# Strassen's form for the first MLP product of layer 0, in a kernel of a two-layer diffusion trunk

## The chip, the cores and the metric

The kernel runs on one core of one Trainium2 chip. The metric is the device time of one execution in microseconds, as the median of the runs. Five engines work side by side, each through its own list of instructions in order: TensorE (PE: matmuls, with its weight loads as PEld), VectorE (DVE), ScalarE (ACT), GpSimd (POOL) and SyncE (SP), which here only issues DMAs. They wait for each other by semaphores.

## The reference

Two layers work on 512 noised tokens and 256 context tokens of 1024 features, all in float32. Each layer has a modulated norm, a combined input projection, a gated mixer and attention, an output projection with a gated residual, and then the MLP:

```python
def sqrelu_mlp(h, w1, w2):
    return jnp.square(jax.nn.relu(h @ w1)) @ w2
...
        x_lat = x_lat + ga2 * sqrelu_mlp(modulate(rmsnorm(x_lat, norm2_g[l]), sh2, sc2),
                                         w_ff1[l], w_ff2[l])
```

`w1` is 1024 x 4096 and `w2` 4096 x 1024. Layer 0 does the same for the context tokens. Layer 1, the last one, needs of the context only its keys and values, so of the context's six modulation vectors it uses only the first two (`csh1`, `csc1`). The output is the noised stream.

## The kernel before

**Number format.** Every float32 operand of a matmul is split into a high part (rounded by an ACT cast) and a low part (the rest, a subtraction). A product is three passes: high x high, high x low, low x high. `split` (lines 206 to 208) does this for a source: `act.copy` on line 207, the subtraction on DVE, or where it is named on POOL, on line 208. Nearly all matmuls go through the helper `mm`, whose matmul is on line 203.

**Layout.** Features lie on the 128 partitions and tokens on the free axis: `X` is the residual stream, `h2[k]` (k = 0 to 7) the normed tokens of a layer's MLP as [128, high/low, 768]. A hidden tile `H[m]` (m = 0 to 31) has the same shape. The tile framework gives each tile a buffer of its tag's pool: units `A0` to `A7`, `B0` to `B6`, `C0`, `C1` and `X0` to `X3` with one buffer each, small temporaries `w` and `s` with three each, and in PSUM `pa` (two banks wide), `pb` and `pt` (one bank), two buffers each. A tile waits for the last reader of the buffer that it takes over.

**Weights.** `pump` (line 224) loads blocks of [128, 1024] through SP (line 242) into two `raw` buffers, in the order that `block_order` (line 120) lists, and splits them into a ring of four pairs of buffers `hi` and `lo`. `take` hands out the next block; `release` lets the ring go on some time later.

**The MLP.** `ff1_first` (line 963) makes hidden tiles 0 to 3, the context's tokens ahead of the noised ones. `ff1(m)` (line 986) makes one hidden tile: two token parts of 384 columns, each 8 feature blocks x 3 passes, 48 matmuls in all. `relu2` (line 951) then takes ReLU and square on ACT (lines 954 and 959) and square and low half on DVE (lines 960 and 961). The second product, `proj4` (line 786), adds four hidden tiles to all 8 output tiles in a chunk: 8 x 2 parts x 12 matmuls. DVE adds each result, times a gate, to `X` (line 784). `steady` (line 1012) runs eight chunks: for `ch` below 7 first `ff1(ch*4+4)`, then the second product of chunk `ch`, then the other three tiles of the next chunk. So a hidden tile of the next chunk stands on PE between the last tile of a chunk and the chunk's second product.

**Beside it**, in layer 0's MLP, `mod_wide` (line 347) computes layer 1's modulation without PE: 12 chunks of 512 columns, each 8 feature blocks for two conditions. ACT scales a block (lines 365 and 368), POOL adds it up (line 369), DVE transposes and reduces (lines 380 and 381), and four small matmuls (line 386) end the sum. `more()` advances it in small steps between the pieces of the MLP. `consts(l)` (line 550) loads a layer's constants and makes the rotary tables times the gains (`G`, lines 563 and 564); for layer 1 it is called right after layer 0's `ff1_first`.

**Order.** The program is written along an emission clock (`Flow`), which counts PE's time and emits delayed work when due. What each engine then runs in which order is chosen by the framework's scheduler from its own cost model, except where a manual region keeps the written order. In layer 0's MLP, chunks 0 to 6 are in such a region for DVE and ACT (`PAR["FM0"] = 'DA'`); layer 1's MLP is in the scheduler's order throughout.

```python
        if eng:
            with tc.manual_schedule(engines=eng):
                steady(range(PAR["FC"]))
            with region('ffz%d' % l):
                steady(range(PAR["FC"], 8))
        else:
            steady(range(8))
```

## Time and profile before

| what | value |
|---|---|
| median of 3 runs | 1532.02 us (1531.33 to 1533.99) |
| profiled execution, its own time: the span from its first to its last instruction | 1530.9 us |
| PE busy | 1484.1 us (97%), 8804 matmuls |
| DVE, ACT, POOL busy | 957.4 (63%), 682.6 (45%), 402.0 (26%) us |
| mean granted PE clock | 0.993 |
| moved by DMA | 148.83 MB, mean 97 GB/s |

The profile gives one execution, and no time for it but its span; what lies around the span is seen only by comparing it with the runs. Instructions are grouped by the line that issues them, the engine, the operation and the names of the tiles that they write and read (`lo<-raw,hi`). A group shows its count, its busy time in us, the mean of one in ns, and after the last bar how long the engine was idle before them and whom it waited for. The chain that ended last is followed back from the last instruction, at each step to what released it. A busy PE need not be PE at its peak, since matmuls are pipelined: the distance between the starts of matmuls tells more than their listed length.

### The profile page before, as it was taken

What the parts mean: (1) busy time and instruction counts of PE and PEld (TensorE: products, weight loads), DVE (VectorE), ACT (ScalarE), POOL (GpSimd) and SP (SyncE); (2) the same over time, 40 slices, a digit from 0 to 9 for tenths busy, and PEclk for the clock granted to TensorE, in tenths of its full rate; (3) what the DMA queues carried; (4) which work ended last, traced back from release to release, by engine and by line L of the source; (5) the groups of instructions that cost most, each with busy time, mean ns of one, the idle gap of its engine ahead of it and who ended that gap; (6) DMA issues with size and microseconds to landing.
All of it is one profiled execution on the core that took longest, in us unless ns stands there. A gap on an engine that the chain in (4) does not pass through costs nothing.

```text
span 1530.9 us, 22786 instructions
## 1 busy us (share of the span) xinstructions
PE 1484.1 (97%) x8804; PEld 1321.5 (86%) x8804; DVE 957.4 (63%) x1874; ACT 682.6 (45%) x1142; POOL 402.0 (26%) x362
## 2 busy tenths in 40 slices
PE   6999899999999999999999999998999999999998
PEld 2899686779899999999999998996889888888887
DVE  5868966776855555555555547988796644444443
ACT  3542355564545453545444424535784433322221
POOL 0112320023244545545454603035213000000000
PEclk9999999999999999999999999999999999999999
DMA  9221324321134333333333321221101333332332
GB/s 359 67 74 48 119 91 152 110 83 56 62 108 122 113 123 126 111 118 106 124 109 124 98 68 56 86 80 44 41 1 56 97 96 97 98 97 97 96 98 79
DMA packets 49948, 148.83 MB, mean 97 GB/s; under 512 B 5424, under 2 KB 6832, under 8 KB 49840
## 3 DMA queue, kind: packets, MB, share of 16 engines
q1 hardware_dynamic: 49264, 146.46, 29.9%
q8 instruction: 69, 1.13, 0.3%
q10 hardware_dynamic: 576, 0.92, 0.2%
q14 instruction: 39, 0.32, 0.1%
HBM read 145.26 MB, written 2.10 MB: 96 GB/s over the span
## 4 chain that ended last, share of the span: by engine, by line
PE 82%; DVE 12%; DMA 2%; ACT 2%; issue 1%; POOL 0%; SPq 0%; ACTq 0%; POOLq 0%; DVEq 0%
PE pa L203 51%; PE pb L203 21%; PE pt L844 3%; PE pt L203 3%; PE pb L326 2%; DVE lo L208 1%; DMA X<-in_xT 1%; DMA C<-in_w_mod 1%; DVE X L784 1%; DMA A<-in_w_mod 1%; DVE m L277 1%; PE pt L626 1%; DVE B L961 1%; ACT hi L207 1%; PE pb L865 0%
## 5 line engine op out<-in xcount | busy, mean ns | idle before, releaser
L203 PE MATMUL pa<-A,hi 128*128 128x384 f32 (+2 forms) x1696 | 449.2, 347 | 1.7 <-ACT w L954 0.6
L207 ACT CAST hi<-raw 128x1024 fp32r<-128x1024 f32 x171 | 179.5, 1050 | 409.9 <-PE pa L203 326.3
L208 DVE TENSOR_TENSOR lo<-raw,hi 128x1024 fp32r<-128x1024 f32 x155 | 202.7, 1308 | 215.8 <-ACT hi L207 212.4
L203 PEld LDWEIGHTS pa<-A,hi 128*128 128x128 f32 x1696 | 304.7, 188 | 25.9 <-ACT w L954 1.8
L369 POOL TENSOR_TENSOR C<-C,s 128x512 f32<-128x512 f32 x168 | 240.5, 1463 | 245.0 <-ACT s L368 244.8
L203 PE MATMUL pa<-A,lo 128*128 128x384 f32 (+2 forms) x848 | 293.4, 347 | 1.1 <-DVE lo L208 1.1
L203 PE MATMUL pa<-B,hi 128*128 128x384 f32 (+1 forms) x900 | 246.4, 356 | 4.4 <-DVE X L784 4.4
L203 PEld LDWEIGHTS pa<-B,hi 128*128 128x128 f32 x900 | 162.9, 188 | 21.5 <-DVE X L784 9.2
L784 DVE SCALAR_TENSOR_TENSOR X<-pa,modT,X 128x384 f32<-128x384 f32 (+1 forms) x168 | 88.0, 547 | 143.0 <-PE pa L203 143.0
L203 PEld LDWEIGHTS pa<-A,lo 128*128 128x128 f32 x848 | 159.3, 188 | 12.0 <-DVE lo L208 1.3
L203 PE MATMUL pa<-B,lo 128*128 128x384 f32 (+1 forms) x450 | 158.1, 353 | 0.0
L203 PE MATMUL pb<-B,hi 128*128 128x256 f32 (+2 forms) x600 | 152.3, 340 | 0.4 <-DVE X L784 0.4
L368 ACT ACTIVATE s<-k,silu 128x512 f32<-128x512 f32 x168 | 114.3, 716 | 49.4 <-DMA k<-in_w_mod 27.3
L203 PE MATMUL pb<-hi,A 128*128 128x256 f32 x672 | 126.1, 285 | 0.0
L784 DVE SCALAR_TENSOR_TENSOR X<-pb,modT,X 128x512 f32<-128x512 f32 (+3 forms) x116 | 69.1, 602 | 75.8 <-PE pb L203 75.3
L203 PEld LDWEIGHTS pb<-B,hi 128*128 128x128 f32 x600 | 104.0, 189 | 11.6 <-DVE X L784 1.0
L203 PEld LDWEIGHTS pb<-hi,A 128*128 128x128 f32 x672 | 106.1, 191 | 0.2 <-issue 0.2
L203 PE MATMUL pb<-B,lo 128*128 128x256 f32 (+2 forms) x300 | 101.5, 338 | 0.0
L203 PE MATMUL pb<-lo,A 128*128 128x256 f32 x336 | 95.3, 284 | 0.0
L203 PEld LDWEIGHTS pa<-B,lo 128*128 128x128 f32 x450 | 84.4, 188 | 5.8
L847 DVE TENSOR_TENSOR A<-pt,A 128x384 fp32r<-128x384 f32 (+1 forms) x144 | 73.6, 535 | 16.4 <-ACT A L846 14.4
L846 ACT CAST A<-pt 128x384 fp32r<-128x384 f32 (+1 forms) x144 | 64.6, 469 | 43.3 <-PE pt L844 39.5
(169 smaller groups left out, 2300.3 us busy)
## 6 DMA issues: line engine op xcount, KB each, us to landing
raw<-in_w_ff SPq DMA_DIRECT2D x128, 512.0 KB, 3.5
k<-in_w_mod SPq DMA_DIRECT2D x96, 256.0 KB, 3.0
hi<-in_w_mod SPq DMA_DIRECT2D x32, 512.0 KB, 3.6
raw<-in_w_tok SPq DMA_DIRECT2D x19, 512.0 KB, 3.5
raw<-in_w_out SPq DMA_DIRECT2D x16, 512.0 KB, 3.5
A<-in_w_mod SPq DMA_DIRECT2D x8, 512.0 KB, 9.9
raw<-in_w_u SPq DMA_DIRECT2D x8, 512.0 KB, 3.5
B<-in_w_mod SPq DMA_DIRECT2D x6, 512.0 KB, 10.2
```

What stands on the lines that cost most here:

```text
L203: pe.matmul(out, a, b, start=start, stop=stop)
L207: act.copy(hi, src)
L208: (eng or vec).tensor_tensor(out=lo, in0=src, in1=hi.bitcast(F32), op=ALU.subtract)
L277: vec.tensor_scalar(yi, v.bitcast(I32), -0.5, 1595932665.0, op0=ALU.mult, op1=ALU.add)
L326: pe.matmul(ps[q:q + 32, :], S32[:, k, :], w[:, k2 * 512:(k2 + 1) * 512], start=k < ns, stop=k >= KT - ns)
L368: act.activation(p, w, AF.Copy, scale=s)
L369: pool_e.tensor_tensor(out=a, in0=a, in1=p, op=ALU.add)
L626: pe.transpose(p[:, o:o + 128], stk[:, t, hh, c0:c0 + 128].bitcast(F32), ident)
L784: vec.scalar_tensor_tensor(out=xs, in0=src[:, s - off:e - off], scalar=modT[l][:, i * 8 + m, cond:cond + 1], in1=xs, op0=ALU.mult, op1=ALU ...
L844: pe.transpose(tp_[:, (kt - k0) * 128:(kt - k0) * 128 + 128], p[:, kt * 128:kt * 128 + 128], ident)
L846: act.copy(pth[:, k0:k0 + step, d], src)
L847: vec.tensor_tensor(out=ptl[:, k0:k0 + step, d], in0=src, in1=pth[:, k0:k0 + step, d].bitcast(F32), op=ALU.subtract)
```

## The change

The first product of layer 0 is cut into quadrants: features into two halves of 4 blocks, tokens into two halves of 384, and hidden tiles into pairs (p, p+16). Seven products of quadrant sums (Strassen's form in Winograd's variant) stand in place of eight products. Tiles 0, 16, 1 and 17 are still made the old way, in `ff1_first`; the other 14 pairs in the new `ff1_pair`. This needs:

- **Weight sums** (`factor`): both raw blocks of a pair are loaded, POOL makes four sums of 512 columns, and three and a half blocks are split (`al`, `be`, `ga`, and `q` in a small buffer of its own) where two were. `take` may now hand out blocks out of order.
- **Token sums** (`factors`), once: POOL adds high and low of `h2`, DVE makes four sums per pair of feature blocks, ACT and DVE or POOL split them. The 16 steps are emitted between the pieces of chunk 0's second product. They lie in place of one quadrant of `h2` and in `B0` to `B5`.
- **Recombination** in `ff1_pair`: ACT copies two products out of PSUM (`c1_`, `c5`), DVE reads PSUM and adds (`U2`, `U3`), POOL adds `U3` to `c5`, and ReLU and square become one DVE operation (`sqrelu`) for three quadrants of four. Four of the seven products go into banks that an earlier product or copy has to leave first or that they accumulate into.

The order becomes: chunk 0's second product right after `ff1_first`, then for each further chunk its two pairs and its second product. `proj4` gets `early`, by which the second product starts three output tiles on the first pair's hidden tiles before it needs the last pair's. No manual region is left in this MLP (`FM0 = ""`). `mod_wide` starts after chunk 0, leaves out the context for its chunks 4 to 11, takes other buffers, and its small matmuls are emitted 6 us later on the emission clock. Layer 1's `consts` moves behind the last chunk, and its tables, layer 0's `S32` and the attention's `mix` share new units `H0` to `H3` with the hidden tiles. The hidden blocks of `w_ff2` of layer 0 are reordered on the host to fit. The scratch for software DMA is made smaller.

The diff, cut to its core:

```diff
-       "FM0": 'DA', "FM1": '', "FC": 7, "MP": [0, 1], "YC": [0, 1], "YK": [0], "RM": {}, "WP": ['out1', 'out0'],
+       "FM0": "", "FM1": '', "FC": 7, "MP": [0, 1], "YC": [0, 1], "YK": [0], "RM": {}, "WP": ['out1', 'out0'],
...
+        if l == 0:
+            o += [("ff1", l, m) for m in (0, 16, 1, 17)]
+            for ch in range(8):
+                if ch:
+                    a, b = 2 * ch, 2 * ch + 1
+                    o += [("al", l, a), ("be", l, a), ("al", l, b), ("ga", l, a), ("be", l, b), ("ga", l, b)]
+                o += [("ff2", l, ch, nb) for nb in range(4)]
+            continue
...
+    def factor(key):
+        kind, l, p = key
+        hi, lo = slot()
+        if kind == "al":
+            ra = ring.tile([128, 1024], F32, tag="raw", name=nm("raw"), bufs=2)
+            nc.sync.dma_start(ra, w_ff1[l, p])
+            rb = unit(("B6", "C0")[p % 2], [128, 1536], F32)
+            nc.sync.dma_start(rb[:, 512:1536], w_ff1[l, p + 16])
+            raws[p] = ra, rb
+            split(hi, lo, ra)
+            a11, a12, s2, a21, a22 = ra[:, 0:512], ra[:, 512:1024], rb[:, 0:512], rb[:, 512:1024], rb[:, 1024:1536]
+            tt = pool_e.tensor_tensor
+            tt(out=a11, in0=a11, in1=a21, op=ALU.subtract)
+            tt(out=a21, in0=a21, in1=a22, op=ALU.add)
+            tt(out=s2, in0=a22, in1=a11, op=ALU.subtract)
+            tt(out=a12, in0=a12, in1=s2, op=ALU.subtract)
+        elif kind == "be":
+            split(hi, lo, raws[p][1][:, 0:1024])
+        else:
+            ra, rb = raws.pop(p)
+            split(hi, lo, ra)
+            qh, ql = (ring.tile([128, 512], F32R, tag=t, name=nm(t), bufs=1) for t in ("qh", "ql"))
+            split(qh, ql, rb[:, 1024:1536])
+            ready.append((("q", l, p), qh, ql))
...
         for j in range(12):
-            acc = unit("C1", [128, 2, 512], F32)
+            conds = range(2 if j < 4 else 1)
+            acc = unit("C1", [128, 3, 512], F32)
...
-                            p = tsm([128, 512])
+                            p = tsm([128, 512]) if j < 4 and cond else acc[:, 2 - nprod % 2 * (j > 3), :]
...
+            fl.defer(PAR["MF"], fin)
...
+        def factors():
+            ux = [unit(f"B{i}", [128, 2, 2, 384]) for i in range(6)]
+            def tokens(k):
+                hv = []
+                for kk in (k, k + 4):
+                    v = tw([128, TQ])
+                    pool_e.tensor_tensor(out=v, in0=h2[kk][:, 0, 0:TQ].bitcast(F32), in1=h2[kk][:, 1, 0:TQ].bitcast(F32), op=ALU.add)
+                    hv.append(v)
+                return hv
+            for k in range(4):
...
+                for i, (x, y) in ((0, (b12, b11)), (1, (b22, 0)), (3, (b21, 1)), (2, (b22, b12))):
+                    t[i] = tsm([128, hn])
+                    vec.tensor_tensor(out=t[i], in0=x, in1=t[y] if isinstance(y, int) else y, op=ALU.subtract)
+                    act.copy(dst[i][:, 0], t[i])
+                    (pool_e if i > 1 else vec).tensor_tensor(out=dst[i][:, 1], in0=t[i], in1=dst[i][:, 0].bitcast(F32), op=ALU.subtract)
+                    yield
...
+        def put(m, j, sq):
+            hi, lo = (H[m][:, a, j * hn:(j + 1) * hn] for a in range(2))
+            act.copy(hi, sq)
+            vec.tensor_tensor(out=lo, in0=sq, in1=hi.bitcast(F32), op=ALU.subtract)
...
+            al = take("al", l, p)
+            product(A, al, 0, quad(0, 0), True, True)
+            act.copy(c1_, A)
+            be = take("be", l, p)
+            product(C, be, 512, tsum(0), True, True)
+            act.copy(c5, C)
+            more()
+            product(A, al, 512, quad(1, 0), False, True)
+            release()
+            r = tsm([128, hn])
+            act.activation(r, A, AF.Relu)
+            hd = H[p]
+            act.activation(hd[:, 0, 0:hn], r, AF.Square)
+            tt(out=r, in0=r, in1=r, op=ALU.mult)
+            tt(out=hd[:, 1, 0:hn], in0=r, in1=hd[:, 0, 0:hn].bitcast(F32), op=ALU.subtract)
+            more()
+            product(B, be, 0, tsum(1), True, True)
+            release()
+            tt(out=U2, in0=B, in1=c1_, op=ALU.add)
+            more()
+            product(E, take("q", l, p), 0, tsum(3), True, True)
+            ga = take("ga", l, p)
+            product(B, ga, 0, tsum(2), False, True)
+            tt(out=U3, in0=B, in1=c1_, op=ALU.add)
+            pool_e.tensor_tensor(out=c5, in0=c5, in1=U3, op=ALU.add)
+            t21 = tsm([128, hn])
+            tt(out=t21, in0=E, in1=U3, op=ALU.add)
+            put(p + 16, 0, sqrelu(t21))
+            more()
+            product(C, ga, 512, quad(1, 1), False, True)
+            release()
+            tt(out=U2, in0=C, in1=U2, op=ALU.add)
+            put(p, 1, sqrelu(U2))
+            put(p + 16, 1, sqrelu(c5))
+            more()
...
-        if not last:
-            K1.append(consts(l + 1))
...
-                if ch < 7:
-                    ff1(ch * 4 + 4)
-                    more()
-                R = [H.pop(ch * 4 + kk) for kk in range(4)]
+                if strassen:
+                    if ch:
+                        ff1_pair(2 * ch)
+                        ff1_pair(2 * ch + 1)
+                    R = [H.pop(m) for m in (2 * ch, 2 * ch + 16, 2 * ch + 1, 2 * ch + 17)]
+                    sums = factors() if ch == 0 else iter(())
...
+                if strassen:
+                    if end:
+                        K1.append(consts(l + 1))
```

More of the change, by code (lines that the diff above doesn't have):

```diff
@@ L263, in take @@
     def take(*key):
-        if not ready:
+        if not any(e[0] == key for e in ready):
             settle()
-        k, hi, lo = ready.pop(0)
-        assert k == key, (k, key)
+        i = [e[0] for e in ready].index(key)
+        assert i == 0 or key[0] in ("be", "ga", "q", "al"), (key, ready[0][0])
+        k, hi, lo = ready.pop(i)
         return hi, lo
@@ L375, in mod_wide @@
                     yield
-            part = small(32).rearrange("p (c b) -> p c b", c=2)
-            for cond in range(2):
+            part = small(32, tag="pa", bufs=2).rearrange("p (c b) -> p c b", c=2)
+            for cond in conds:
                 tr = tsm([128, 512])
@@ L532, in trunk, with fm_mms @@
     DENSE = {0: ((0, 384), (384, 384)), 1: ((0, 512),)}
-    def fm_mms(dst, pairs, off, n):
-        tot, i = 3 * len(pairs), 0
-        for whi, wlo, rhi, rlo in pairs:
+    def fm_mms(dst, pairs, off, n, k0=0, k1=None):
+        tot, i = 3 * len(pairs), 3 * k0
+        for whi, wlo, rhi, rlo in pairs[k0:k1]:
             for a, b in ((whi, rhi), (whi, rlo), (wlo, rhi)):
@@ new lines, in put, with sqrelu, product @@
+        def put(m, j, sq):
+            hi, lo = (H[m][:, a, j * hn:(j + 1) * hn] for a in range(2))
+            act.copy(hi, sq)
+            vec.tensor_tensor(out=lo, in0=sq, in1=hi.bitcast(F32), op=ALU.subtract)
+        def sqrelu(t):
+            vec.scalar_tensor_tensor(out=t, in0=t, scalar=0.0, in1=t, op0=ALU.max, op1=ALU.mult)
+            return t
+        def product(dst, w, wo, rhs, first, last_):
+            for k in range(4):
+                whi, wlo = (a[:, wo + k * 128:wo + k * 128 + 128] for a in w)
+                rhi, rlo = rhs(k)
+                for i, (a, b) in enumerate(((whi, rhi), (whi, rlo), (wlo, rhi))):
+                    pe.matmul(dst, a, b, start=first and k == 0 and i == 0, stop=last_ and k == 3 and i == 2, skip_group_check=True)
+                    fl.vt += hn / 2.4 + 13.0
+            fl.tick()
```

131 lines of the change are left out of this document (100 added, 31 removed), and 2 rows, old and new, of the table PAR.

## The prediction

> **What bounds the kernel now.** I read the page's first part and its chain of waits, then the busy time by stretch, then the waits of PE and ACT, then the groups of the stretch that changes.
>
> ```profile
> span 1530.9 us, 22786 instructions
> PE 1484.1 (97%) x8804; PEld 1321.5 (86%) x8804; DVE 957.4 (63%) x1874; ACT 682.6 (45%) x1142; POOL 402.0 (26%) x362
> ...
> PE 82%; DVE 12%; DMA 2%; ACT 2%; issue 1%; POOL 0%; SPq 0%; ACTq 0%; POOLq 0%; DVEq 0%
> ```
>
> The matmuls bound it: PE is busy in 97% of the span and makes 82% of the chain. In the view by stretches (length, then busy time and instruction count of PE, its weight loads, DVE, ACT, POOL; granted clock; DMA) 402 to 437 is the first chunk of layer 0's MLP, 437 to 905 the chunks that follow, and 1190 to 1527 the same loop in layer 1.
>
> ```profile
> 402.00:437.00 35.00, 34.91 (x170) 30.63 (x171) 26.54 (x42) 19.90 (x32) 4.81 (x3) 1.00 0.26 79
> 437.00:905.00 468.00, 463.56 (x2717) 454.51 (x2716) 250.34 (x340) 218.81 (x293) 235.64 (x166) 1.00 0.37 114
> 955.00:1005.00 50.00, 50.00 (x334) 45.80 (x332) 42.90 (x139) 25.48 (x46) 4.57 (x6) 1.00 0.30 95
> 1005.00:1055.00 50.00, 43.02 (x321) 40.04 (x320) 47.69 (x123) 19.11 (x30) 26.14 (x17) 0.98 0.21 64
> 1190.00:1527.00 337.00, 336.95 (x1523) 279.77 (x1522) 164.19 (x200) 99.49 (x128) 0.00 (x0) 1.00 0.30 96
> ```
>
> In 437 to 905 PE lacks only 468.00 - 463.56 = 4.4 us. So what is taken off PE there comes off the time, as long as the other engines still answer PE in time. Chain rows (start, length) and waits (total, times, longest):
>
> ```profile
> 573.28 1.92 DVE B L961
> ...
> 665.13 33.52 PE pa L203 x192
> ...
> 1022.89 2.31 DVE m L280
> ```
> ```profile
> PE pa L203 <- DVE X L784: 4.4, 5, 1.2
> ```
> ```profile
> ACT hi L207 <- PE pa L203: 129.7, 35, 8.4
> ...
> ACT s L368 <- DMA k<-in_w_mod: 27.3, 19, 2.8
> ```
> ```profile
> DVE lo L208 <- ACT hi L207: 102.3, 32, 6.2
> ```
>
> The 192 matmuls are four hidden tiles of the first product: 33.52 / 192 = 0.1746 us each. The 4.4 us are five waits at chunk starts, where the chain passes through the last low half of a hidden tile (DVE B, line 961). The chain leaves PE only past 1005, where DVE is busy for 47.69 of 50 us.
>
> **The change, part by part.** (1) *Fewer matmuls.* A pair of hidden tiles (p, p+16) took 8 quadrant products of 4 feature blocks x 3 passes, 96 matmuls 384 wide; the new form takes 7, 84 matmuls. Width and passes stay, so 0.1746 us holds. The first four tiles keep the old form, so 14 pairs save 14 x 12 x 0.1746 = **-29.3 us**. The second product and layer 1 keep their matmuls.
>
> (2) *Load of the other engines*, which must stay below PE's some 440 us. Rows of 470 to 905, of all POOL groups, of layer 1's loop, and of PSUM reads 384 wide (line 846 ACT, line 847 DVE):
>
> ```profile
> L208 DVE TENSOR_TENSOR lo<-raw,hi 128x1024 fp32r<-128x1024 f32 x51 | 74.0, 1451 | 102.3 <-ACT hi L207 102.3
> L961 DVE TENSOR_TENSOR B<-w,B 128x768 fp32r<-128x768 f32 x23 | 34.7, 1510 | 0.8
> L960 DVE TENSOR_TENSOR w<-w 128x768 f32<-128x768 f32 x26 | 24.9, 956 | 7.9 <-ACT B L959 7.2 <-ACT C L959 0.7
> ...
> L380 DVE STREAM_TRANSPOSE s<-C 128x512 f32<-128x512 f32 x22 | 15.4, 701 | 0.0
> L381 DVE TENSOR_REDUCE m<-s 128x16 f32<-128x512 f32 x22 | 15.1, 685 | 0.8
> ```
> ```profile
> L368 ACT ACTIVATE s<-k,silu 128x512 f32<-128x512 f32 x152 | 103.1, 716 | 44.6 <-DMA k<-in_w_mod 27.3 <-POOL C L369 17.1
> L207 ACT CAST hi<-raw 128x1024 fp32r<-128x1024 f32 x52 | 54.5, 1048 | 137.4 <-PE pa L203 129.7 <-PE pt L203 7.6
> L954 ACT ACTIVATE w<-pa 128x768 f32<-128x768 f32 x26 | 20.9, 803 | 0.0
> L959 ACT ACTIVATE B<-w 128x768 fp32r<-128x768 f32 x23 | 19.5, 849 | 0.7
> ```
> ```profile
> L369 POOL TENSOR_TENSOR C<-C,s 128x512 f32<-128x512 f32 x168 | 240.5, 1463 | 245.0 <-ACT s L368 244.8
> ...
> L208 POOL TENSOR_TENSOR B<-s,B 128x512 fp32r<-128x512 f32 x6 | 7.7, 1291 | 42.2 <-ACT B L207 25.8 <-issue 16.5
> ...
> L775 POOL TENSOR_TENSOR A<-C,A 128x768 fp32r<-128x768 f32 x2 | 4.1, 2062 | 1.5 <-ACT A L774 1.5
> ...
> L614 POOL TENSOR_TENSOR k<-w,k 128x256 fp32r<-128x256 f32 x3 | 2.4, 809 | 35.1 <-ACT k L613 35.1
> ```
> ```profile
> L208 DVE TENSOR_TENSOR lo<-raw,hi 128x1024 fp32r<-128x1024 f32 x60 | 73.5, 1225 | 94.3 <-ACT hi L207 91.2
> ...
> L961 DVE TENSOR_TENSOR B<-w,B 128x512 fp32r<-128x512 f32 x24 | 16.6, 691 | 0.8
> ...
> L961 DVE TENSOR_TENSOR B<-w,B 128x256 fp32r<-128x256 f32 x8 | 3.2, 418 | 0.1
> ```
> ```profile
> L847 DVE TENSOR_TENSOR A<-pt,A x144: 385/547/559, 187.8 to 1146.7; 128x384 fp32r<-128x384 f32 x128, 128x256 fp32r<-128x256 f32 x16
> ```
> ```profile
> L846 ACT CAST A<-pt x144: 370/479/497, 187.4 to 1146.2; 128x384 fp32r<-128x384 f32 x128, 128x256 fp32r<-128x256 f32 x16
> ```
>
> Operations 384 wide in SBUF I estimate midway between the 256 and 512 wide rows: DVE 0.555, POOL 1.05 us.
> POOL: 8 chunks of the modulation lose their context half, -8 x 7 x 1.463 = -81.9; weight sums 14 x 4 x 1.291 = +72.3; one sum a pair, 14 x 1.05 = +14.7; token sums 8 x 2.062 + 8 x 1.05 = +24.9. 235.6 becomes 266, 60% of 440.
> DVE: -8 x (0.701 + 0.685) = -11.1. A pair took 2 x (1.451 + 0.956 + 1.510) = 7.8; now it takes three splits and a half one (5.04), four reads of PSUM (2.19) and eight 384-wide operations (4.44), 11.7: 14 x 3.9 = +54; token sums 24 x 0.555 = +13. 250 becomes 306, 70%.
> ACT: -64 x 0.716 = -45.8; a pair goes from 2 x (1.048 + 0.803 + 0.849) = 5.4 to 3.5 casts of weights (3.67) and 7 x 0.479 = 7.0, +23; token sums 16 x 0.479 = +8. 219 becomes 204, 46%.
> None becomes the bound, so this costs 0 in the sum, hidden under PE's 440 us; past 440, each further us of an engine would be a us of the time.
> DVE's split of weights takes 1.451 us here and 1.225 in layer 1's loop, where POOL does nothing. [...]
>
> (3) *Waits at chunk starts.* The new second product starts three output tiles on the hidden tiles of the first pair: 36 matmuls, 36 x 0.1746 = 6.3 us, ahead of what needs the last pair. That tail is two sums and squares (3 x 0.55), two low halves (2 x 0.555 to 2 x 0.96, L960's time for twice the width) and two casts (2 x 0.48), 3.7 to 4.5 us, so it is covered. Of the 4.4 us I take **-4.0** (bounds -4.4 and 0).
>
> (4) *After the first chunk*
>
> ```profile
> L959 ACT ACTIVATE B<-w 128x512 fp32r<-128x512 f32 x24 | 15.2, 634 | 0.8
> ```
>
> no hidden tile follows that would cover the last two squares: ACT 4 x 0.634 and DVE 0.69 + 0.69 on 512 tokens come to some 3.9 us, against two hidden tiles that are ready, which give between 6 matmuls (1.0 us) and, over several output tiles, 36 (6.3). Bounds 0 and +2.9; I take **+1.0**, nearer to cover, because PE's order is the scheduler's.
>
> (5) *Token sums under the first second product* (16 groups, 192 x 0.1746 = 33.5 us). POOL has 24.9 us of them and 2 x 4 x 1.291 = 10.3 of the first two pairs' weight sums, 35.2 in all; the last low half is due five products (5 x 2.1 us) later, at 44. With POOL slower by half it would be at 53, 9 late. Bounds 0 and +9; I take **+1.5**. PE's product waits, and behind it all of PE.
>
> (6) *Waits within a pair.* The third product accumulates into the bank that ACT must have copied (c1), the sixth into the bank that DVE must have read (U2), each with one product, 12 x 0.1746 = 2.1 us, of cover. ACT: one cast ahead (1.048) and the copy (0.479), 1.5. DVE: one split ahead (1.451) and the sum (0.547), 2.0. So mostly covered, with no room. Behind a late one stand PE's next products and, through c1, DVE's U2 and U3. Bounds 0 and, two waits a pair of 1 us each, +28; I take 0.3 a pair, **+4.2**, nearer to the two covered rows.
>
> (7) *Constants of layer 1* move from the first chunk to the end of the MLP, into units of the hidden tiles, so their loads (ACT's queue, and the spatial weights on SP's) wait for the last matmul on those.
>
> ```profile
> 950.45 0.40 PE L203 MATMUL pb<-C,hi 128*128 128x256 f32 x2
> ```
> ```profile
> DMA to landing us min/median/max: 3.3/3.3/3.3
> ```
> ```profile
> L563 DVE TENSOR_TENSOR G<-w,k x8: 278/280/283, 4.7 to 432.6; 128x128 f32<-128x128 f32 x8
> ...
> L597 DVE TENSOR_TENSOR w<-pa,G x4: 408/412/417, 62.4 to 957.6; 128x256 f32<-128x256 f32 x4
> ```
>
> The last such matmul stands at 950.5, the load lands 3.3 us later (line 556's row), eight operations of 0.28 follow: ready at about 956.5 plus a few small ones, and the first reads of G end the kernel's list at 957.6, so up to 2 us late, with some 3 us of DVE work more where it is busy for 42.90 of 50. Behind it waits ACT's queue, and PE for the PSUM banks of the first projection. The next stretch is DVE's, so what is added may stay. Bounds 0 and +5; I take **+1.5**. (8) The last pair's cover is only 18 matmuls: **+0.5** (0 to 1). Renamed tiles (S32, mix, the DMA scratch) I put at 0, -0.5 to +1: no row of theirs is on the chain.
>
> Sum: -29.3 - 4.0 + 1.0 + 1.5 + 4.2 + 1.5 + 0.5 = -24.6, so a span of 1506.3. The span stands 1.1 us under the median of the runs (1532.02), which covers what lies around it: **1507.4 us**.
>
> **The rivals.** [...] DVE is 70% busy and its two-input operations stretch beside POOL (1.510 for 768 wide, against 0.691 x 1.5 = 1.04). If two such stand ahead of U2, it comes after 2 x 1.51 + 0.55 = 3.6 us, 1.5 past its cover, in each pair: 14 x 1.5 = 21 in place of 4.2, **1524**. Against it: 30% of DVE stays free.
>
> *Queues that stand at a wait: slower than before.* ACT and DVE execute in order, and now stand long at single instructions: a cast waits 129.7 / 35 = 3.7 us for its slot, a split 102.3 / 32 = 3.2 for the cast. Today nothing short hangs on that. If the scheduler puts c1's copy behind such a cast, the third product is late by 3.7 + 0.5 - 2.1 = 2.1, and U2 behind such a split by 3.2 + 0.55 - 2.1 = 1.65: 3.75 a pair, 14 x 3.75 = 52 on the 1503.2 without pair waits, **1556**. It decides from (1532.0 - 1503.2) / 14 = 2.06 us a pair on; just there the time would not change. Against it: layer 1's loop is in the scheduler's order and lacks 0.05 us of 337; for it: that loop has no POOL work and no such short waits.
>
> *Token sums late, and the clock.*
>
> ```profile
> 1053.86 1.65 PE L203 MATMUL pa<-B,B 128*128 128x512 f32 x4 [4.24 <-ACT w L828]
> ```
> ```profile
> 1050.00:1060.00 10.00, 6.14 (x16) 4.94 (x17) 6.76 (x15) 2.92 (x5) 5.11 (x5) 0.66 0.25 78
> ```
>
> Behind an idle 4.24 us the granted clock fell to 0.66 over 10 us, 3.4 us of work lost. If step (5) comes to such a wait: 4.4 + 3.4 in place of 1.5, **1514**. [...]
>
> **How the numbers follow.** The forecast 0.62; the interface 0.14; the late sums 0.07; standing queues 0.17, of which 0.05 lie about the point where nothing changes. A kernel like this can be told from no change at 0.2%, 3 us. Faster 0.62 + 0.14 + 0.07 = 0.83, same 0.05, slower 0.12. The range goes from all gains without any price (1532.0 - 29.3 - 4.4 = 1498) to just past the interface rival, 1529; outside lie the 0.17 of the standing queues.
>
> **What would show it.** Step 1: 168 matmuls fewer on PE, at the same 0.17 us each. Step 3: no wait at the chunk starts. Steps 4, 5: gaps of PE within 20 us of the first chunk's end and at the first pair's second to sixth products. Step 6: PE's waits in the pairs named on ACT's copy and DVE's U2, near 4 us in all. Step 7: the first projection of layer 1 waiting for G. POOL near 266, DVE near 306, ACT near 204 us in this loop. Wrong would make it: waits in the pairs of over 2 us each, a loop in which DVE or POOL is busy throughout, or a stretch after the MLP that is as much longer as the MLP is shorter.

## The result, and the profile after

The changed kernel takes **1591.63 us** (median; 1591.29 to 1592.18) against 1531.9 us before on the same chip: a ratio of 1.0385 (95% interval 1.0371 to 1.0400), some 60 us slower, where 1507.4 us was forecast.

From the first part and the chain of the changed kernel's page:

```profile
span 1589.5 us, 22579 instructions
PE 1485.5 (93%) x8636; PEld 1312.0 (83%) x8636; DVE 1035.8 (65%) x2022; ACT 669.6 (42%) x1164; POOL 434.9 (27%) x392
...
PE 46%; DVE 14%; POOL 5%; ACT 4%; issue 3%; DMA 1%; POOLq 0%; ACTq 0%; DVEq 0%
```

PE lost the 168 matmuls that were to go (8804 to 8636), and yet is busy as long as before: part of what is left runs at a lower rate (mean granted clock 0.975, against 0.993 before). No engine is above 65% except PE, and PE's share of the chain fell from 82% to 46%. The chain now runs through PE, DVE and POOL in turn.

The loss has one place. The first matmul of layer 1's key and value projection starts at 940.5 us before and at 996.8 after: +56.4 of the span's +58.6. Of the rest, 1.5 lies between there and layer 1's attention, 0.7 in that attention, and nothing behind it. From the starts of PE's matmuls in layer 0's MLP I worked out how long PE stood and how much went at half rate: 18.9 us and 0 before (400 to 952), 82.9 and 22.5 after (400 to 1012). So -29.3 for the matmuls, +64.0 for standing, +22.5 for the clock: +57.2.

By stretches of the changed MLP (columns as in the prediction: length; busy time and count of PE, weight loads, DVE, ACT, POOL; granted clock; DMA):

```profile
437.00:560.00 123.00, 97.59 (x497) 94.50 (x497) 80.73 (x110) 49.05 (x77) 82.87 (x60) 0.88 0.23 75
560.00:680.00 120.00, 105.22 (x578) 101.38 (x577) 71.95 (x105) 54.73 (x84) 62.68 (x46) 0.91 0.35 111
680.00:962.00 282.00, 264.60 (x1496) 254.08 (x1495) 171.72 (x264) 103.72 (x155) 119.39 (x89) 0.98 0.33 106
437.00:962.00 525.00, 467.40 (x2567) 449.96 (x2567) 324.39 (x477) 207.50 (x315) 264.94 (x193) 0.94 0.31 100
```

The loads are those of the prediction: POOL 265 (266 forecast), ACT 208 (204), DVE 324 (306). In 525 us no engine but PE is above 62%. The loss is densest in the first 240 us, where the clock is lowest too. What PE and DVE wait for there (total, times, longest), from the waits of 402 to 980:

```profile
PE pa L211 <- DVE X L840: 45.2, 16, 8.2
...
DVE s L430 <- POOL C L419: 20.4, 4, 9.7
...
PE pa L1116 <- ACT w L1136: 11.9, 6, 5.2
```

L840 is the gate that empties a bank of the second product, L430 the transpose in `mod_wide`, L419 POOL's sum of the modulation, L1136 the copy `c1_`. PE waits 45 us for gates, and DVE stands only 20 us at transposes, but one event shows how the second leads to the first. POOL around 540 us:

```profile
533.00 1.30 POOL L419 TENSOR_TENSOR C<-C,s 128x512 f32<-128x512 f32 x1
534.26 1.28 POOL L288 TENSOR_TENSOR raw<-raw,B 128x512 f32<-128x512 f32 x1
...
541.79 1.27 POOL L419 TENSOR_TENSOR C<-C 128x512 f32<-128x512 f32 x1
```

DVE in the same time (in brackets the idle time ahead and its releaser):

```profile
532.78 0.62 DVE L840 SCALAR_TENSOR_TENSOR X<-pa,modT,X 128x384 f32<-128x384 f32 x1 [0.22 <-PE pa L211]
543.09 0.71 DVE L430 STREAM_TRANSPOSE s<-C 128x512 f32<-128x512 f32 x1 [9.70 <-POOL C L419]
544.32 0.71 DVE L430 STREAM_TRANSPOSE s<-C 128x512 f32<-128x512 f32 x1 [0.51 <-POOL C L419]
544.95 0.70 DVE L840 SCALAR_TENSOR_TENSOR X<-pa,modT,X 128x128 f32<-128x128 f32 x2
545.57 1.22 DVE L216 TENSOR_TENSOR lo<-B,hi 128x1024 fp32r<-128x1024 f32 x1
546.70 0.61 DVE L840 SCALAR_TENSOR_TENSOR X<-pa,modT,X 128x384 f32<-128x384 f32 x1
```

And PE:

```profile
547.37 1.01 PE L211 MATMUL pa<-H,hi 128*128 128x384 f32 x2 [8.16 <-DVE X L840]
```

At 533.4 DVE is done with a gate, and next in its order stands a transpose of a modulation sum. POOL still has that sum to finish, and between its adds it has weight sums of the next pair (L288). It ends at 543.1. For 9.7 us DVE does nothing, while gates that PE needs are queued behind the transpose: DVE does both transposes, three gates and a split before PE gets its bank at 547.3. DVE and PE are both idle, and neither is overloaded. In the written order of before, the transposes stand where POOL has long delivered: 22 of them, with 0.0 us of idle ahead (L380, 470 to 905).

Most such stands cost once more afterwards, in the clock. PE after another one:

```profile
468.76 1.01 PE L211 MATMUL pa<-H,hi 128*128 128x384 f32 x2 [6.15 <-DVE X L840]
...
470.85 0.84 PE L211 MATMUL pa<-H,hi 128*128 128x384 f32 x2
...
471.81 0.84 PE L211 MATMUL pa<-H,hi 128*128 128x384 f32 x2
...
475.95 0.51 PE L211 MATMUL pa<-H,hi 128*128 128x384 f32 x2
...
476.47 0.51 PE L211 MATMUL pa<-H,hi 128*128 128x384 f32 x2
```

Between 470.85 and 471.81 lie three matmuls, 0.32 us each; between 475.95 and 476.47 three as well, 0.173 each, though one alone is listed at 0.34 there: listed lengths overlap. For some 5.5 us after an idle 6.15 PE works at about half its rate. All such phases of this MLP, twelve of them by the granted clock, come to 64.9 us, in which 22.5 us of work are lost. Five follow stands of 4.7 to 8.2 us, but seven follow stands of only 1.8 to 2.6 us, and two more stands of 1.9 and 2.3 us brought none. So the length of a stand alone does not tell whether such a phase follows; what does, the trace does not show.

Not every wait of PE has this cause. Followed back through the trace, its 16 waits of over 1.4 us (54.3 of the 61 us that the view of waits lists) split so:

- Two, 16.4 us, lead to a transpose that stands for POOL, as above.
- Three, 5.6 us, lead to a split whose cast is late because ACT stood for POOL's modulation sums, with a gate behind the split.
- Four, 11.7 us, lie in chunk 0, where DVE has the token sums among its gates and stands for POOL's part of them.
- Two, 9.9 us, are for `c1_`: ACT has it behind casts that wait for DVE's squares.
- Five, 10.8 us, come soon after the start of a second product. There DVE stood for nobody. It was at work on the last pair's squares and low halves, and the gate came behind them:

```profile
756.99 3.18 DVE L1105 TENSOR_TENSOR H<-w,H 128x384 fp32r<-128x384 f32 x2
...
760.16 0.60 DVE L840 SCALAR_TENSOR_TENSOR X<-pa,modT,X 128x384 f32<-128x384 f32 x1
```
```profile
760.91 0.98 PE L211 MATMUL pa<-H,hi 128*128 128x384 f32 x2 [2.28 <-DVE X L840]
```

These two low halves took 3.18 us, and POOL was at two modulation adds meanwhile (from 756.77 and 758.29). The same operation just ahead of them, begun while POOL stood still, took 0.54, and without the modulation (after_nomod below) all of them take 0.55. So operations of DVE that are slowed beside POOL have a share of the loss as well.

### The profile page after: what moved, and what is told of

Same layout as the page of the kernel before. It is cut to its first block, busy times and chain, and to the rows that moved or that the text cites. A ratio compares the mean times of both kernels' runs of the same rounds, so it can differ in the third digit from the quotient of the medians.

```text
span 1589.5 us, 22579 instructions
## 1 busy us (share of the span) xinstructions
PE 1485.5 (93%) x8636; PEld 1312.0 (83%) x8636; DVE 1035.8 (65%) x2022; ACT 669.6 (42%) x1164; POOL 434.9 (27%) x392
## 4 chain that ended last, share of the span: by engine, by line
PE 46%; DVE 14%; POOL 5%; ACT 4%; issue 3%; DMA 1%; POOLq 0%; ACTq 0%; DVEq 0%
PE pa L211 26%; PE pb L211 10%; PE pa L1116 5%; DVE lo L216 3%; POOL C L419 2%; PE pb L1116 2%; ACT hi L215 2%; DVE w L1108 1%; PE pt L211 1%; PE pt L924 1%; DMA k<-in_w_mod 1%; DVE H L1105 1%; DVE X L840 1%; DVE H L1148 1%; DVE s L1147 1%
## 5 line engine op out<-in xcount | busy, mean ns | idle before, releaser
L211 PE MATMUL pa<-H,hi 128*128 128x384 f32 (+1 forms) x688 | 189.7, 360 | 48.3 <-DVE X L840 45.2
L211 PE MATMUL pa<-A,hi 128*128 128x512 f32 (+2 forms) x800 | 221.0, 362 | 2.6 <-DVE B L708 0.8
L211 PEld LDWEIGHTS pa<-H,hi 128*128 128x128 f32 x688 | 129.7, 200 | 59.6 <-DVE X L840 40.2
L840 DVE SCALAR_TENSOR_TENSOR X<-pa,modT,X 128x384 f32<-128x384 f32 (+2 forms) x170 | 89.3, 548 | 123.4 <-PE pa L211 123.0
L419 POOL TENSOR_TENSOR C<-C 128x512 f32<-128x512 f32 x84 | 122.6, 1459 | 107.6 <-ACT C L418 105.4
L211 PE MATMUL pa<-A,lo 128*128 128x512 f32 (+2 forms) x400 | 143.4, 360 | 1.1 <-DVE lo L216 1.1
L1116 PE MATMUL pa<-A,hi 128*128 128x384 f32 x448 | 119.7, 348 | 11.9 <-ACT w L1136 11.9
L211 PE MATMUL pa<-H,lo 128*128 128x384 f32 (+1 forms) x344 | 119.1, 352 | 0.0
L840 DVE SCALAR_TENSOR_TENSOR X<-pb,modT,X 128x512 f32<-128x512 f32 (+3 forms) x114 | 67.6, 599 | 69.2 <-PE pb L211 68.8
L211 PE MATMUL pb<-B,hi 128*128 128x512 f32 (+1 forms) x404 | 101.2, 341 | 0.1
L211 PE MATMUL pa<-B,hi 128*128 128x512 f32 x300 | 92.4, 389 | 0.0
L211 PEld LDWEIGHTS pa<-A,lo 128*128 128x128 f32 x400 | 75.3, 189 | 11.9 <-DVE lo L216 1.3
```

The source lines that it names most:

```text
L211: pe.matmul(out, a, b, start=start, stop=stop)
L419: pool_e.tensor_tensor(out=a, in0=a, in1=p, op=ALU.add)
L840: vec.scalar_tensor_tensor(out=xs, in0=src[:, s - off:e - off], scalar=modT[l][:, i * 8 + m, cond:cond + 1], in1=xs, op0=ALU.mult, op1=ALU ...
L1116: pe.matmul(dst, a, b, start=first and k == 0 and i == 0, stop=last_ and k == 3 and i == 2, skip_group_check=True)
```

## The experiments

Three explanations ran against each other; the expectations call them A, B and C. A: an engine that executes in order stands still and waits for POOL, and what PE needs is queued behind it. B: load, of DVE or of DVE and POOL together, or Strassen's own work. C: waits within the pairs. All runs were compared with the kernel before on the same chip.

| run | us | ratio to before (95%) |
|---|---|---|
| before_sched | 1589.1 | 1.0359 [1.0314, 1.0404] |
| after_da | 1640.21 | 1.0692 [1.0646, 1.0737] |
| after_d | 1615.55 | 1.0544 [1.0523, 1.0565] |
| before_nomod | 1521.92 | 0.9931 [0.9904, 0.9959] |
| after_nomod | 1526.18 | 0.9955 [0.9940, 0.9970] |
| after_moddve | 1543.22 | 1.0067 [1.0047, 1.0088] |
| after_halfadd | 1558.4 | one run |
| after_nomod_tok | 1514.76 | 0.9882 [0.9862, 0.9901] |
| after_moddve_tok | 1529.91 | 0.9986 [0.9977, 0.9996] |
| after_moddve_tok_even | 1533.01 | 1.0000 [0.9989, 1.0012] |
| after_mp1_tok | 1543.17 | 1.0071 [1.0054, 1.0088] |
| after_d_tok | 1618.11 | 1.0561 [1.0530, 1.0591] |
| before_cond | 1530.11 | 0.9985 [0.9975, 0.9994] |
| before_sched_moddve | 1532.47 | 0.9993 [0.9983, 1.0004] |
| before_cond_sched_moddve | 1532.62 | 0.9995 [0.9984, 1.0005] |
| before_cond_moddve | 1546.66 | 1.0086 [1.0071, 1.0101] |

### The order alone, in the kernel before

```diff
-       "FM0": 'DA', ...
+       "FM0": "", ...
```

> The kernel before with one value changed: VectorE and ScalarE of layer 0's MLP in the scheduler's order instead of the written one. Theory A (standing queue): in the scheduler's order DVE stands at the modulation's transposes until POOL has added up, with the gate operations that empty PSUM behind it, and PE waits; this needs no Strassen, so the time rises, to 1545 to 1600 us, with DVE idle before its transposes for POOL. [...] Theory C (waits within the pairs): 1530 to 1535 us, since there are no pairs here.

1589.1 us: **57 us slower with no Strassen in it**, nearly all of the change's loss. Waits of this kernel, 402 to 980:

```profile
DVE s L380 <- POOL C L369: 32.0, 17, 6.2
ACT s L368 <- POOL C L369: 28.4, 37, 4.4
...
PE pa L203 <- DVE X L784: 17.1, 12, 3.3
PE pa L203 <- ACT w L954: 16.0, 4, 5.8
```

The same transposes stand for POOL's sums (L380 for L369), 32 us in all, and PE stands for DVE's gates (L784). ACT comes late as well: it waits 28.4 us for POOL to free what it scales into, and PE for its ReLU (L954). One of PE's waits has another cause: the longest, 5.84 us at 430, is for the ReLU, which ACT reaches late because it stood for the modulation's weights:

```profile
428.61 1.33 ACT L368 ACTIVATE s<-k,silu 128x512 f32<-128x512 f32 x2 [4.87 <-DMA k<-in_w_mod]
```

The work is that of before, and so are its loads, 437 to 962:

```profile
437.00:962.00 525.00, 489.11 (x2748) 476.03 (x2748) 255.96 (x352) 213.91 (x285) 225.82 (x155) 0.95 0.31 101
```

DVE at 256 of 525 us and POOL at 226 are half idle: neither is fuller here than before (250 and 236 of 468 us, 437 to 905), where the time is 57 us less.

### The written order, in the changed kernel

```diff
-       "FM0": "", ...
+       "FM0": 'DA', ...
```

> The changed kernel with one value changed back: VectorE and ScalarE of this MLP in the written order for chunks 0 to 6. Theory A: the transposes and gates come as written, most of the waits at the second products go, 1510 to 1550 us. Theory B: the same work on the same engines, 1580 to 1600 us. Theory C: the written order puts the pair's copies no nearer, 1575 to 1600 us.

1640.21: a clear miss of what A expected, and above what B and C expected. The order as the change writes it is worse than the scheduler's. PE's waits (402 to 1010) moved into the pairs:

```profile
PE pa L1116 <- ACT w L1136: 36.3, 12, 7.0
PE pb L1116 <- ACT hi L215: 25.1, 8, 3.5
PE pa L211 <- DVE X L840: 9.3, 5, 3.2
```

and of ACT's groups, 437 to 1010, the one that it stands at longest (busy and mean, then the idle time ahead):

```profile
L215 ACT CAST hi<-B 128x1024 fp32r<-128x1024 f32 x7 | 7.3, 1045 | 62.1 <-POOL B L290 62.1
```

This is the cast of `be`, which contains POOL's third weight sum (L290). POOL can begin these sums only when DVE has split `al`, and then has four to do among the modulation's adds; ACT, in written order, waits up to 12.0 us for them, with the copy `c1_` behind it, and PE behind that. So what hurts is not the scheduler's order as such: here a written order, too, lets an engine that PE depends on reach a POOL result before POOL has delivered it. With DVE alone in written order:

> The changed kernel with DVE alone in the written order for chunks 0 to 6, ACT in the scheduler's. With both in the written order PE waited 61 us for ACT in the pairs (copies and casts) and 9 us for the gates on DVE; with both in the scheduler's 45 us for the gates and 12 us for ACT. Theory A: the gates' waits go with DVE's order, the copies' with ACT's, so the mix gets the better of each, 1530 to 1560 us. Theory B: order moves the waits about but the load decides, 1580 to 1640 us.

1615.55, missed by A too, in B's range. Waits of 402 to 980:

```profile
ACT hi L215 <- POOL B L290: 68.0, 7, 13.1
DVE lo L216 <- ACT hi L215: 56.6, 17, 9.7
...
PE pb L1116 <- ACT hi L215: 24.0, 6, 7.8
```

ACT stands at the same cast, though nothing prescribes its order now, and DVE, which has to take its splits in written order, stands behind ACT.

### POOL's modulation taken away

These two leave out layer 1's modulation (`mod_wide`): its vectors are the constant 0.5.

```diff
-        wide = None if last else mod_wide(l + 1)
+        wide = None
...
+        pool_e.memset(t_, 0.5)
```

> The kernel before without the modulation of layer 1 (its values are set to a constant, so the work beside layer 0's MLP is left out). All theories: PE lacks only 4.4 us there, so 1522 to 1532 us. It is the partner of the next run.

> The changed kernel without the modulation of layer 1 (set to a constant). Theory A: POOL is left with the weight and token sums, DVE has nothing of the modulation to stand at; the time falls below before's, to 1495 to 1512 us, PE's waits in the MLP under 15 us. Theory B: POOL has about 110 us left of 266, so it falls too, but DVE's load is nearly the same and its stretched operations stay, 1515 to 1540 us. Theory C: the pairs keep their waits, 1560 us and more.

1521.92 and 1526.18: without this work the changed kernel's loss falls from 60 us to 4.3 over its partner, but no gain appears: 1526.18 is above A's range and inside B's. In it PE stands some 33 us in the MLP and loses some 4 to the clock. One stand is the largest, from the waits of 402 to 932:

```profile
PE pa L211 <- DVE X L842: 11.6, 4, 6.2
...
PE pa L1118 <- ACT w L1138: 3.6, 7, 0.5
```

It lies in chunk 0's second product, and what DVE does ahead of the gate shows why:

```profile
457.18 2.18 DVE L1098 TENSOR_TENSOR s<-w,s 128x384 f32<-128x384 f32 x1 [2.47 <-POOL w L1087]
...
465.55 1.33 DVE L1098 TENSOR_TENSOR s<-w,s 128x384 f32<-128x384 f32 x1 [1.70 <-POOL w L1087]
```

POOL's token sums (L1087) are late, DVE stands at them twice, and gates are behind: A's mechanism again with other work. DVE's own work on the sums stands ahead of the gates too; the run that takes these sums off POOL (after_nomod_tok below) tells the two apart. In chunk 0 PE stands 13.5 us, and the loss to the clock lies there too.

### The modulation's sums on DVE

```diff
-       "FM0": "", ..., "MP": [0, 1], ...
+       "FM0": "", ..., "MP": [], ...
```

> The changed kernel with the modulation's sums on DVE alone (scale and add in one DVE operation) in place of ACT and POOL: the same numbers, POOL 163 us less, DVE some 90 us more, so DVE is busy for about 400 of 440 us. Theory A (DVE stands in order behind what POOL has not finished): nothing of the modulation waits for POOL, so in spite of the load the time falls, to 1535 to 1560 us. [...] Theory C (waits within the pairs): as now or worse, 1590 to 1610 us.

The sums go to DVE together with ACT's scalings, as one operation each. 1543.22: **48 us faster than the changed kernel, by giving DVE more work** (437 to 905):

```profile
437.00:905.00 468.00, 444.90 (x2525) 430.17 (x2526) 358.04 (x584) 124.89 (x187) 118.82 (x82) 0.97 0.32 106
```

DVE is busy for 358 of 468 us (76%, against 62% in the changed kernel). DVE's busy time as such is excluded as the cause: a fuller DVE that takes these sums itself is better than an emptier one beside POOL. The edit also leaves POOL less to do beside DVE (119 of 468 us busy, against 265 of 525), and DVE's squares and low halves fall back to 0.55 us, from 1.03 and 0.97. By before_sched a loss of this size needs no more load than before; but how much of the 48 us is DVE no longer standing and how much its operations no longer being slowed, no run separates.

> The changed kernel, in which POOL leaves out three of the seven additions of each modulation sum (so layer 1's modulation is not the reference's); ACT's scalings, DVE's transposes and everything else stay. Theory A: POOL keeps up, DVE no longer stands at the transposes, 1530 to 1555 us, DVE's idle time before the transposes under 5 us. Theory B: DVE's load is unchanged, 1575 to 1592 us. Theory C: 1585 to 1592 us.

```diff
+                            if k % 2:
-                                pool_e.tensor_tensor(out=a, in0=a, in1=p, op=ALU.add)
+                                pool_e.tensor_tensor(out=a, in0=a, in1=p, op=ALU.add)
```

With three of POOL's seven adds a sum left out: 1558.4 in a single run, just above A's range and well below B's. Less work for POOL shortens the stands and does not end them: 16.1 us of DVE's waiting at transposes are left, of 20.4, where A expected under 5.

### Token sums on DVE as well

```diff
-                    pool_e.tensor_tensor(out=v, in0=h2[kk]...
+                    vec.tensor_tensor(out=v, in0=h2[kk]...
...
-                    (pool_e if i > 1 else vec).tensor_tensor(out=dst[i][:, 1], ...
+                    vec.tensor_tensor(out=dst[i][:, 1], ...
```

> The changed kernel without layer 1's modulation, as before, and with the token sums and their low halves on DVE alone instead of partly on POOL. In that kernel chunk 0 lost some 14 us of idle PE and 6 us to the lower clock. Theory A: these come from DVE standing at token sums that POOL has not made; on one engine nothing is waited for, so 1526 falls to 1508 to 1518 us, though DVE does some 12 us more in chunk 0. Theory B: DVE's load in chunk 0 is the limit, so it rises to 1530 to 1540 us.

1514.76, 11.4 us less than after_nomod: the step of chunk 0 is confirmed. This is the first changed kernel that beats its partner (before_nomod, 1521.92), by 7.2 us of the 29.3.

> The changed kernel with both repairs: the modulation's sums and the token sums on DVE, POOL left with the weight sums and one sum a pair. Theory A (DVE stands in order behind POOL): the two gains add, 1543.2 - 11.4 = 1532 us, 1528 to 1536. Theory B (load): DVE now has all of it and PE waits for DVE, 1540 us and more.

1529.91: with all the work of the changed kernel, 62 us faster than it, and some 2 us faster than before by the interval, though within the 0.2% that the prediction calls no change. Of the listed waits of PE (402 to 930)

```profile
PE pa L211 <- DVE X L840: 12.7, 9, 3.2
...
PE pa L1116 <- ACT w L1136: 1.6, 3, 0.6
```

the gates keep 12.7 us. Spreading the modulation's steps more finely and evenly

```diff
+                    if k and cond == 0 and len(conds) > 1:
+                        yield
...
-                    if n % 2 == 1 and not end and ch:
+                    if n % 4 != 3 and not end and ch:
```

> As the last, with the modulation in finer and more even steps: a step after each condition in the four chunks that have two, and twelve steps instead of eight beside each second product. Theory A: DVE's burst in chunks 1 and 2, beside which PE lost three waits of 3.1 to 3.3 us, is halved, 1522 to 1530 us, which would be faster than both kernels. Theory B: the same load, the same time as the last within 3 us.

gave nothing (1533.01), a miss. With only the context's half of the modulation left on POOL (`"MP": [1]`, chunks 0 to 3 of `mod_wide`):

> The repaired changed kernel (1529.9 us) with the context's sums, in the first four chunks alone, back on ACT and POOL. PE lost 3.1 and 3.4 us there in DVE's bursts. Theory A: DVE stands at the context's four transposes again for POOL, 1530 to 1545 us. Theory B: DVE's load falls where it was highest, 1522 to 1528 us.

1543.17: a few sums on POOL bring 13 us back. The time is in A's range, but not by A's mechanism, for DVE hardly stands at the transposes (402 to 945):

```profile
DVE s L430 <- POOL C L419: 1.3, 2, 0.9
```

PE's listed waits grow by some 9 us, spread over gates, copies and ReLUs; what makes them late was not tried. And the token sums moved in after_d:

> The last with the token sums on DVE. Theory A: some 10 us less than the last, as without the modulation; Theory B: no less.

1618.11, no gain where 10 us were expected: there ACT at `be` is the wait.

### What Strassen's form is worth by itself

The change also leaves out work: the context half of 8 chunks of the modulation. In the kernel before, by itself (written order):

```diff
-                for cond in range(2):
+                for cond in range(2 if j < 4 else 1):
...
```

> The kernel before with one part of the change alone: the modulation of layer 1 leaves out the context for its chunks 4 to 11, where no result uses it. In the written order PE lacked 4.4 us in the MLP, and leaving out the whole modulation gave 10.6 us. All theories: half of the sums gone gives 3 to 7 us, 1525 to 1529 us; if the change's loss came from this part, the time would rise instead.

1530.11: worth about 2 us, less than the 3 to 7 expected. Next the scheduler's order in the kernel before, without POOL's sums (`"FM0": ""`, `"MP": []`), and the same with the context half left out, which is after_moddve_tok without Strassen's form:

> The kernel before in the scheduler's order (which took 1589.1 us), with the modulation's sums on DVE instead of ACT and POOL. If the scheduler's order is slow because of what waits for POOL, as theory A has it, 1535 to 1555 us, as in the changed kernel; if it is slow by itself, 1580 us and more.

> As the last, and without the context half of the modulation's chunks 4 to 11. It is the repaired changed kernel (1529.9 us) without Strassen's form. If the form's 168 matmuls fewer are worth what the pairs' waits and the token sums leave of them, this takes 8 to 18 us more than 1529.9: 1538 to 1548 us. If the form brings nothing, 1526 to 1533 us.

1532.47 and 1532.62, both at the time before; the first is below the range expected. So **the 57 us of before_sched go when the modulation's sums leave POOL and its scalings leave ACT**; the scheduler's order by itself costs nothing that can be measured. The run does not part POOL's sums from ACT's scalings, one of which made the 5.84 us wait above. Waits of PE in before_sched_moddve:

```profile
PE pa L203 <- DVE X L784: 5.1, 7, 1.8
```

Against before_cond_sched_moddve, after_moddve_tok is 2.7 us faster by the medians, which come from two chips, and 1.4 us by the ratios to before, whose intervals overlap. So Strassen's form, once order is out of the way, is worth 1 to 3 us at most and not clearly anything; 1532.62 lies where the expectation says that the form brings nothing. Rows 480 to 930 of the one without it,

```profile
480.00:930.00 450.00, 446.40 (x2576) 434.85 (x2575) 242.61 (x366) 98.18 (x110) 7.76 (x6) 1.00 0.31 100
```

and of after_moddve_tok:

```profile
480.00:930.00 450.00, 436.95 (x2519) 419.19 (x2518) 341.51 (x572) 125.16 (x187) 100.22 (x70) 1.00 0.34 113
```

DVE goes from 243 to 342 us, and PE lacks 13 us of 450 in place of 3.6. From the starts of the matmuls over the whole MLP, PE stands 16.9 us without the form and 38.4 with it, and loses 1.3 us more to the clock: some 23 of the 29 us go there. Another 4 go behind the MLP: key and value projection to attention +1.7, attention +2.5.

Last, the DVE sums in the written order:

> The kernel before in its written order with the modulation's useful part alone (1530.1 us), its sums on DVE instead of ACT and POOL. DVE has some 90 us more, but POOL no longer stretches DVE's splits and low halves; without the modulation this kernel took 1521.9. Theory A: PE's waits at the chunk starts came from DVE's low halves, so 1523 to 1528 us. Theory B: DVE's load counts, 1531 to 1540 us.

1546.66, above both ranges. The load is not the reason, for before_cond_sched_moddve does the same work on the same engines in 1532.62: what differs is the order. In the order written for sums on POOL, PE waits for gates 14.4 us in 13 places.

## Why the prediction was wrong

**The step that failed** is the sentence that closed step (2): "None becomes the bound, so this costs 0 in the sum, hidden under PE's 440 us". Its loads held to 1, 18 and 4 us. But load was the wrong question for engines that execute in order and wait for each other. What `FM0 = ""` moved is the place in DVE's order at which POOL's sums are awaited, and that term stood at 0. In the kernel before it is 57 us by before_sched, and by before_sched_moddve all of it hangs on the modulation's sums on POOL and their scalings on ACT. In the changed kernel the loss is 64.0 us of standing PE and 22.5 of half clock, less the 29.3 of matmuls, and 62 us go when the modulation's and the token sums move to DVE (after_moddve_tok). DVE's slowed operations have a part in it that no run sets apart. The prediction's own rows had the missing hint: POOL's modulation group with 245 us of idle ahead of it shows that POOL worked just in time behind ACT, and the transposes with 0.0 us of idle ahead show that the written order placed them late enough. I read that 0.0 as a property of the work, and it was one of the order.

**Step (1)** held: 168 matmuls fewer, at 0.173 us where the clock is whole. That they come off the time did not: PE was no longer what the MLP waits for.

**Step (3)** failed too in the changed kernel. It covered the last pair's tail of 3.7 to 4.5 us with 6.3 us of matmuls, with low halves of 0.555 to 0.96 us. In the rows above two low halves took 3.18 us, and the gate whose bank PE needed stood behind them in DVE's order. The prediction's own row names that gate (`DVE X L784`), where the step spoke of the low half alone. In place of -4.0 there are the five waits of 10.8 us.

**Steps (3), (4) and (6)** look better where POOL is not late. PE's waits of after_nomod_tok, 402 to 921:

```profile
PE pa L1118 <- ACT w L1138: 3.1, 6, 0.5
PE pa L211 <- DVE X L842: 2.8, 2, 1.8
PE pb L1118 <- DVE w L1154: 1.0, 1, 1.0
```

Within the pairs they are 3.1 for `c1_` and 1.0 for `U2`, 4.1 us where step (6) put 4.2 (in the changed kernel `c1_` alone has 11.9). Chunk starts have no waits over 1 us left there, as step (3) had it; the 2.8 lie in chunk 0. For step (4) stands this wait of the changed kernel, at the end of the first chunk, 1.2 us against +1.0:

```profile
432.03 0.44 PE L211 MATMUL pa<-H,hi 128*128 128x384 f32 x1 [1.17 <-DVE H L1041]
```

**Step (5)** was right that the token sums come late and wrong in who waits: not "PE's product" on its operand, but PE on a bank whose gate stands in DVE's order behind a token subtraction. By after_nomod it is 13.5 us and some 4 of clock, above the +9 of its bound; 11.4 us came back when the sums left POOL.

**Step (7)** put +1.5 on the constants: the stretch from layer 1's key and value projection to its attention became 1.5 us longer in the changed kernel, and 4.2 in after_nomod against before_nomod. Size and bounds fit; which wait makes it was not tried, so the fit may be luck. The 1.1 us that the sum adds around the span set a median against another execution's span; in one and the same execution it is 1.8 (1591.29 against 1589.5).

**The rivals.** The standing queues had the mechanism, an engine that stands at an instruction with short work queued behind, at 0.17 and at 1556. Their own place, `c1_` behind a cast of ACT, made 9.9 us in two pairs, where they put 3.75 us into each of 14. More came from places that they did not name: DVE at a transpose or a token sum, with the second product's gates behind. "Layer 1's loop is in the scheduler's order and lacks 0.05 us of 337" was counted against them, though the same sentence says why it could not be: that loop has no POOL work, so its order has nothing to stand at. The order itself, which the change names in its text, had deserved its own term and the largest chance of loss. The rival at 0.14 and 1524, with DVE's operations stretched beside POOL, had a real effect, though no run shows an interface that the two share: on 384 columns DVE's square takes 1.03 us and its low half 0.97 beside a busy POOL (470 to 962 of the changed kernel),

```profile
L1108 DVE SCALAR_TENSOR_TENSOR w<-w 128x384 f32<-128x384 f32 x27 | 27.5, 1032 | 4.5 <-POOL w L1158 4.5
L1105 DVE TENSOR_TENSOR H<-w,H 128x384 fp32r<-128x384 f32 x26 | 24.7, 968 | 0.1
```

and the same square 0.55 where POOL has no modulation (after_nomod, 470 to 930):

```profile
L1110 DVE SCALAR_TENSOR_TENSOR w<-w 128x384 f32<-128x384 f32 x28 | 15.5, 554 | 8.3 <-POOL w L1160 8.3
```

Against the 0.555 of the estimate that is 27 x 0.477 + 26 x 0.413 = 23.6 us, enough for the 18 us by which DVE's load was forecast too low. DVE was not full for it, but it shows in the 10.8 us at the chunk starts. The clock rival's mechanism was right (half the rate behind stands), and as a multiplier of every other stand it is worth 22.5 us, not the 3.4 of one.

**What stays open.** Why the scheduler set DVE's transposes ahead of POOL's sums was not seen: nothing in a trace tells what it reckoned with. Of the 38 us that PE still stands in after_moddve_tok's MLP the gates name 12.7 and other listed waits 5.5, and the rest is made of small gaps that were not taken apart; in after_nomod_tok, too, the MLP is only 10 us shorter than in before_nomod, with some 9 us of listed waits and some 3 lost to the clock, and so some 8 us go in gaps that no wait explains. Layer 1's attention takes 91.1 to 92.0 us in the changed kernel and in nearly all of its variants and 89.1 to 90.4 in the forms without Strassen, first to last exponential; that `mix` now shares a buffer with a hidden tile may be why, and was not tried.

## What to carry to other kernels

Before costing work as hidden because no engine is full, list for each engine in order what it waits for and what is queued behind it: engines at 50 and 62% that wait for each other in turn stopped the third here. A change from a written to a scheduled order is an edit of its own with its own price, to be looked for at every result that comes from a slow engine (here POOL, with 1.46 us for an add of 512 columns, where DVE in after_moddve scales and adds in 0.87), and can be tried out by moving that result onto the engine that needs it. Fewer matmuls are worth only what remains when the extra work around them has been fed in time: of 29.3 us here, 1 to 3, which the noise hardly lets one see.

## What was not expected

More work on DVE made the kernel faster: it went from 62% to 76% busy and the time fell by 48 us. And standing costs more than the standing: in the changed kernel 64 us more of it brought 22.5 us at half rate on top. The rate of that is not fixed: 59.6 us of standing cost 18.4 in before_sched, 62.4 cost 8.9 in after_halfadd, and some 33 cost some 4 in after_nomod. What decides it was not tried.
